# A decoder layer: the second norm's rows scaled and turned again, the up projection as one 512-column product

## The chip, the cores and the metric

The kernel runs on one core of a Trainium2 chip. The metric is the device time of one execution in microseconds, as the median of several runs. Profiled executions give a trace with every instruction of every engine: TensorE (PE in the rows, with its weight loads as PEld), VectorE (DVE), ScalarE (ACT), GpSimd (POOL) and SyncE (SP).

## What is computed

One layer of a hybrid decoder on 256 tokens of 1024 channels, in float32. Three attention branches are gated, merged, projected and added to `x`. Then comes the part that the change is in, a convolutional feed-forward block with 2 x 2816 inner channels:

```python
x = x + merged @ w_out[l]
h2 = rmsnorm(x, ffn_norm_g[l])
u = causal_depthwise_conv(h2 @ w_ffn_up[l], ffn_conv_w[l], ffn_conv_b[l])   # width 3
u_gate, u_val = jnp.split(u, 2, axis=-1)
x = x + (jax.nn.silu(u_gate) * u_val) @ w_ffn_down[l]
```

## The kernel before

**Split numbers.** TensorE multiplies rounded float32 (`F32R`). To keep the precision of float32, each operand is split into a high part (a rounded copy, made on ACT) and a low part (the rest, made on VectorE), and each product is done as three: high x high, high x low, low x high. All three are summed in PSUM. The low x low part is left out.

**Weights.** Every weight is loaded in pieces of up to 1024 columns a partition (`raw`, 6 buffers), and ACT copies it to `hi` (6 buffers, 8 in the feed-forward part). The low part `lo` is made in one of two ways: VectorE subtracts (`split_lo("dve")`), or ACT writes the negated high part and a DMA from POOL's queue adds `raw` to it (`split_lo("sum")`, the POOL rows of line 374). The second way is open to a piece only if its first use lies at least `SUMS[2]` = 5 units of work ahead (lines 339 to 347).

**Order.** The kernel is written by a planner that runs as the program is built (`Order`, lines 155 to 234). Work is a set of tasks, each a chain of stages on named engines. The planner has a cost for each instruction, takes at each step the engine that can start earliest, and there the stage with the smallest priority number among those that are due. So each engine's queue is in a fixed order, and on the chip it is worked off strictly in that order. The matmuls of the projections are the `spine`, units in a fixed sequence with priority 50; turns of rows, normalisation and evacuation are other tasks that are set between. PSUM has 4 accumulator banks (`acc`), 2 for turns (`tp`) and a larger one (`sc`). A unit that opens an accumulator waits until the fourth before it is free.

**Before the feed-forward block.** The output projection writes `x` in rows (tokens on partitions): columns 0 to 511 for both halves t = 0, 1 of the tokens, then columns 512 to 1023 of t = 0, then of t = 1. `resid` adds it to `xs`. `sums` and `rstd_task` give 1/rms of each row (`rs_h`, its power on POOL).

**The normalised input, twice.** The up projection wants channels on partitions. `turn` transposes the unscaled rows of `xs` on TensorE (`tp_hu`), and ACT and VectorE write them, times the norm's gain (a column factor), as high and low part into `T["hu"]`. The scaling by 1/rms is then by token, which lies along the free dimension: `R` holds it on all partitions, made by a product of ones with a diagonal (`tp_Rh`). Groups c < `RAW` = 3 (a group is two f of 128 channels, for gate s = 0 and value s = 1) use `T["hu"]` and multiply the accumulator by `R` afterwards (lines 979 to 981). Later groups use `T["h"]`, which `scale_task` (lines 910 to 922) makes for each k from `hu`: POOL adds the two parts (`y_h`), VectorE multiplies by `R`, ACT and VectorE split again.

**Up projection and convolution.** `up_unit` multiplies, for one f and s, k0 to k1 of the eight k; `chan` (lines 801 to 807) issues for each k three matmuls of 256 columns into one half of a bank. The first groups are cut in k so that they can start early. `conv_task` (lines 977 to 1001) then takes the accumulator: ACT scales and adds the bias (`y`), two VectorE products add the tokens one and two back, and the bank is free. SiLU (s = 0), the product of both sides and its split into `gT` follow.

**Down projection.** `dn_units` multiplies `gT` with `w_ffn_down` in 512-column matmuls (in the second half of the columns, t = 1 as two of 256), and `store` adds the result to `xs` and writes it out.

All instructions that go through the planner's wrapper have line L105 in the profile, so tiles tell them apart.

Of the kernel before, what the change touches and what calls it, by code (L numbers as in the profile page):

```python
# [11 lines left out]
F32 = mybir.dt.float32  # L12
# [3 lines left out]
AF = mybir.ActivationFunctionType  # L16
ALU = mybir.AluOpType
# [3 lines left out]
P = 128  # L21
S = 256
NT = 2
D = 1024
KT = D // P
# [9 lines left out]
NSLOT = 6  # L35
NRAW = 6
WARM = 4
RAW = 3
PRIO_SCALE = 11
CUTS = (0, 1, 2, 4, 6, 8)  # L40
LOADS = "x02 g w w x24 w X46 w X68 w"
SUMS = (4, 130, 5)
# [195 lines left out]
def tile_layer(ctx: ExitStack, tc: tile.TileContext, io, out):  # L238
    nc = tc.nc
    od = Order(nc)  # L240
    pe, act, dve, pool = od.pe, od.act, od.dve, od.pool
# [10 lines left out]
    def bank_free(tag):  # L252

        return lambda: users[tag][-BANKS[tag]]["end"] if len(users[tag]) >= BANKS[tag] else 0.0

    def bank(tag, name):
        use = {"end": None}
        users[tag].append(use)
        shape = [P, 2, 512] if tag == "sc" else [P, 512]
        return ps.tile(shape, F32, tag=tag, name=name, bufs=BANKS[tag]), use  # L260
# [11 lines left out]
    grain_of = {}  # L272
# [21 lines left out]
    at = {"unit": 0, "raw": 0, "dma": 0.0, "sw": 0.0, "lo": 0, "quiet": False}  # L294
# [44 lines left out]
    def next_lo(eng):  # L339

        for g in grains[at["lo"]:]:
            if g.get("hi", {"end": None})["end"] is None:
                return None
            if not g.get("taken"):
                if eng == "dve":
                    return g
                return g if SUMS[0] <= g["id"] < SUMS[1] and g["first"] - at["unit"] >= SUMS[2] else None

    def take_lo(eng):
        g = next_lo(eng)  # L350
# [60 lines left out]
    xs = cpool.tile([P, NT, D], F32, tag="xs", name="xs")  # L411
    small = cpool.tile([P, 3 * KT + HALF + NT], F32, tag="small", name="small")
    gcol = small[:, :3 * KT].rearrange("p (g k) -> p g k", g=3)
# [4 lines left out]
    ident = cpool.tile([P, P], F32, tag="ident", name="ident")  # L418
# [3 lines left out]
    sq, rstd = {}, {}  # L422
# [6 lines left out]
    def done(*keys):  # L429

        return lambda: [task.get(k, {"end": None}) for k in keys]
# [369 lines left out]
    def chan(o, g, cs, T_, ks, first=True, final=True):  # L801

        for n, (i, k) in enumerate(ks):
            hi, lo = g["hl"][0][:, i, cs], g["hl"][1][:, i, cs]
            pe.matmul(o, hi, T_[:, k, 0, :], start=first and n == 0, stop=False)
            pe.matmul(o, hi, T_[:, k, 1, :], start=False, stop=False)
            pe.matmul(o, lo, T_[:, k, 0, :], start=False, stop=final and n == len(ks) - 1)

    def gate_evac(c, acc, use):
        sl = sig[:, 2 * c:2 * c + 2, :]  # L810
        yield Stage("act", frees=[use])
        act.activation(sl, acc.rearrange("p (i s) -> p i s", i=2), AF.Copy)
        yield Stage("pool", done("R0", "R1"))
        pool.tensor_tensor(sl, sl, R.unsqueeze(1).to_broadcast([P, 2, S]), op=ALU.mult)
# [92 lines left out]
            dve.tensor_add(xc, acc[:, i * w:(i + 1) * w], xc)  # L907
            task[("r", t, c, i)] = {"end": od.t["dve"] + od.HOP}

    def scale_task(k):  # L910

        hi, lo = (T["h"][:, k, i, :] for i in range(2))
        a, b = (T["hu"][:, k, i, :].bitcast(F32) for i in range(2))
        y = f_["y"][:, k, :]
        yield Stage("pool", done(*[("hu", t, k // 2 * 2) for t in range(NT)]))
        pool.tensor_tensor(y, a, b, op=ALU.add)
        yield Stage("dve", done(("R", 0), ("R", 1)))
        dve.tensor_mul(y, y, R)
        yield Stage("act")
        act.activation(hi, y, AF.Copy)  # L920
        yield Stage("dve")
        dve.tensor_sub(lo, y, hi.bitcast(F32))

    def wo_units(c):
        hold = {}
        seq = [(t, k) for k in range(0, KT, 2) for t in range(NT)] if c == 0 else \
            [(t, k) for t in range(NT) for k in range(0, KT, 2)]

        def emit(t, k0):
            def go():  # L930
                if t not in hold:
                    hold[t] = bank("acc", f"acc_o{c}_{t}")
                if c == 1 and t == 0 and k0 == 0:
                    open_ffn()
                    for i in range(NT):
                        turn(xs[:, i, :], "hu", i, 1, 6, lambda k, i=i: done(("r", i, 0)), groups=((0, 2), (2, 4)))
                g = grain_of[("wo", c, k0, 0)]
                ts = slice(t * P, (t + 1) * P)
                for i in range(2):
                    mm3(hold[t][0], (T["m"][:, k0 + i, 0, ts], T["m"][:, k0 + i, 1, ts]),  # L940
                        (g["hl"][0][:, i, :], g["hl"][1][:, i, :]), k0 + i == 0, k0 + i == KT - 1)
                if k0 == KT - 2:
                    task[("r", t, c)] = od.add(resid(t, c, *hold[t]), -2 if c else 12)
                    row = xs[:, t, :]
                    if c == 0:
                        sums(row, "h", t, 14, [(0, 512, "act", done(("r", t, 0)))])
                        return
                    n = 2 if t else 1
                    sums(row, "h", t, -1, [(512, 768, "act", done(("r", t, 1, 0))),
                                           (768, 1024, "dve", done(("r", t, 1, n - 1)))])  # L950
                    at["quiet"] = t == 1
                    turn(row, "hu", t, 1, -1.5, lambda k0: done(("r", t, 1, (k0 - 4) // 2 if t else 0)),
                         groups=((4, 6), (6, 8)))
                    task["rs", "h", t] = od.add(rstd_task("h", t), -1)
                    task["R", t] = od.add(row_scale_task("h", t), 2)
                    for k in range(KT if t else 0):
                        task["h", k] = od.add(scale_task(k), PRIO_SCALE)
            return go
        for t, k0 in seq:
            unit(emit(t, k0), [("wo", c, k0, 0)], done(*[("mg", 2, ct) for ct in (k0,)]), opens=k0 == 0)  # L960
# [7 lines left out]
    def open_ffn():  # L968
        apool_cm.__exit__(None, None, None)
        f_["pool"] = ctx.enter_context(tc.tile_pool(name="fpool", bufs=1))  # L970
        for key in ("hu", "h"):
            T[key] = f_["pool"].tile([P, KT, 2, S], F32R, tag="T_" + key, name="T_" + key)
        f_["y"] = f_["pool"].tile([P, KT, S], F32, tag="y", name="y_h")
        f_["g"] = [None, None, f_["pool"].tile([P, NF - 2 * KT, 2, S], F32R, tag="gT", name="gT")]
        rings["x"] = {"pool": f_["pool"], "n": 2, "of": []}

    def conv_task(f, s, acc, use, raw):
        cw = conv[:, s * NF + f, :]
        if raw:
            yield Stage("dve", done(("R", 0), ("R", 1)))  # L980
            dve.tensor_mul(acc, acc, R)
        yield Stage("act")
        y = f_["pool"].tile([P, S], F32, tag=f"y{s}", name=f"y{s}_{f}", bufs=2)
        act.activation(y, acc, AF.Identity, scale=cw[:, 2:3], bias=cw[:, 3:4])
        yield Stage("dve", frees=[use])
        dve.scalar_tensor_tensor(y[:, 1:], acc[:, :S - 1], cw[:, 1:2], y[:, 1:], op0=ALU.mult, op1=ALU.add)
        dve.scalar_tensor_tensor(y[:, 2:], acc[:, :S - 2], cw[:, 0:1], y[:, 2:], op0=ALU.mult, op1=ALU.add)
        if s == 0:
            yield Stage("act")
            act.activation(y, y, AF.Silu)  # L990
            f_[("y", f)] = y
        else:
            yield Stage("dve", done(("u", f, 0)))
            if f % KT == 0 and f < 2 * KT:
                f_["g"][f // KT] = tpool.tile([P, KT, 2, S], F32R, tag="T8", name=f"gT{f // KT}")
            g = f_["g"][f // KT][:, f % KT]
            dve.tensor_mul(y, f_[("y", f)], y)
            yield Stage("act")
            act.activation(g[:, 0, :], y, AF.Copy)
            yield Stage("dve")  # L1000
            dve.tensor_sub(g[:, 1, :], y, g[:, 0, :].bitcast(F32))

    def up_unit(f, s, k0, k1, raw):
        def go():
            if k0 == 0:
                f_["acc", f, s] = bank("acc", f"acc_u{f}_{s}")
            acc, use = f_["acc", f, s]
            acc = acc[:, :S]
            chan(acc, grain_of[("up", f, s, 0, 0)], slice(0, P), T["hu" if raw else "h"],
                 [(k, k) for k in range(k0, k1)], k0 == 0, k1 == KT)  # L1010
            if k1 == KT:
                task[("u", f, s)] = od.add(conv_task(f, s, acc, use, raw), 10)
        unit(go, [("up", f, s, 0, 0)],
             done(*([("hu", t, k) for t in range(NT) for k in range(k0, k1, 2)] if raw else
                    [("h", k) for k in range(k0, k1)])), opens=k0 == 0)
# [198 lines left out]
```

## Time and profile before

| | us |
|---|---|
| median of 3 runs | 415.3 (414.57 to 415.33) |
| the profiled execution's own time | 414.52 |
| its span, first to last instruction | 412.7 |
| TensorE busy | 404.2 |
| VectorE busy | 302.5 |
| ACT busy | 271.6 |
| POOL busy | 60.5 |

The profiled execution is at the low end of the runs, and 1.8 us of it lie around the span. Busy shares are averages over stages. A matmul's row is longer than its distance to the next, since matmuls are pipelined; the starts tell what one costs.

### The profile page before, as it was taken

What the parts mean: (1) busy time and instruction counts of PE and PEld (TensorE: products, weight loads), DVE (VectorE), ACT (ScalarE), POOL (GpSimd) and SP (SyncE); (2) the same over time, 40 slices, a digit from 0 to 9 for tenths busy, and PEclk for the clock granted to TensorE, in tenths of its full rate; (3) what the DMA queues carried; (4) which work ended last, traced back from release to release, by engine and by line L of the source; (5) the groups of instructions that cost most, each with busy time, mean ns of one, the idle gap of its engine ahead of it and who ended that gap; (6) DMA issues with size and microseconds to landing.
All of it is one profiled execution on the core that took longest, in us unless ns stands there. A gap on an engine that the chain in (4) does not pass through costs nothing.

```text
span 412.7 us, 7727 instructions
## 1 busy us (share of the span) xinstructions
PE 404.2 (98%) x2948; PEld 381.6 (92%) x2948; DVE 302.5 (73%) x601; ACT 271.6 (66%) x449; POOL 60.5 (15%) x62
## 2 busy tenths in 40 slices
PE   7999999999999999999999899999999999999996
PEld 6999999989989999999889799999999999888986
DVE  3998996576886676468978999999997778545301
ACT  5789755879985766957676959676677776443200
POOL 0002361313233212212017000000000000000000
PEclk9999999999999999999999999999999999999999
DMA  8999987577278786687696769667789688654001
GB/s 260 369 312 343 321 231 225 128 203 192 67 179 220 194 220 170 152 245 203 191 270 162 193 143 246 192 191 217 222 253 230 214 241 239 202 185 143 1 2 51
DMA packets 97557, 82.74 MB, mean 200 GB/s; under 512 B 2928, under 2 KB 85488, under 8 KB 97520
## 3 DMA queue, kind: packets, MB, share of 16 engines
q1 hardware_dynamic: 94784, 73.33, 59.6%
q0 software_dynamic: 2448, 8.39, 11.1%
q10 hardware_dynamic: 288, 0.52, 0.5%
q8 instruction: 23, 0.38, 0.4%
q14 instruction: 14, 0.11, 0.1%
HBM read 72.80 MB, written 1.05 MB: 179 GB/s over the span
## 4 chain that ended last, share of the span: by engine, by line
PE 93%; ACT 2%; DVE 2%; DMA 1%; issue 0%; SPq 0%; ACTq 0%
PE acc_u L105 27%; PE acc_g L105 17%; PE acc_d L105 15%; PE acc_o L105 5%; PE acc_qd L105 2%; PE acc_bd L105 2%; PE acc_va L105 2%; PE acc_ba L105 2%; PE acc_kd L105 2%; PE acc_qa L105 2%; PE acc_vd L105 2%; PE acc_ka L105 2%; PE sc L105 2%; PE po L105 2%; PE acc_qm L105 1%; PE acc_mk L105 1%
## 5 line engine op out<-in xcount | busy, mean ns | idle before, releaser
L105 PE MATMUL acc_u<-T_h,hi_up 128*128 128x256 f32 x512 | 91.4, 282 | 0.0
L105 PEld LDWEIGHTS acc_u<-T_h,hi_up 128*128 128x128 f32 x512 | 78.9, 189 | 0.0
L105 PE MATMUL acc_u<-T_h,lo_up 128*128 128x256 f32 x256 | 72.1, 282 | 0.0
L105 PE MATMUL acc_g<-T_x,hi_gate 128*128 128x256 f32 x384 | 71.6, 287 | 0.0
L105 PEld LDWEIGHTS acc_g<-T_x,hi_gate 128*128 128x128 f32 x384 | 59.6, 191 | 2.1 <-issue 1.8
L105 PE MATMUL acc_d<-hi_dn,gT 128*128 128x512 f32 (+1 forms) x220 | 57.0, 348 | 0.0
L105 PE MATMUL acc_g<-T_x,lo_gate 128*128 128x256 f32 x192 | 54.2, 282 | 0.0
L105 ACT ACTIVATE hi_up<-raw_up 128x1024 fp32r<-128x1024 f32 x44 | 46.0, 1053 | 3.9 <-PE acc_o L105 1.7
L105 PEld LDWEIGHTS acc_u<-T_h,lo_up 128*128 128x128 f32 x256 | 48.4, 189 | 0.0
L105 DVE TENSOR_TENSOR lo_up<-raw_up,hi_up 128x1024 fp32r<-128x1024 f32 x39 | 47.6, 1232 | 0.0
L105 DVE SCALAR_TENSOR_TENSOR y<-acc_u,conv,y 128x255 f32<-128x255 f32 x88 | 42.2, 481 | 7.3 <-ACT y L105 5.4
L105 PEld LDWEIGHTS acc_d<-hi_dn,gT 128*128 128x128 f32 x220 | 38.5, 189 | 5.6
L105 DVE TENSOR_TENSOR lo_dn<-raw_dn,hi_dn 128x1024 fp32r<-128x1024 f32 x21 | 25.7, 1224 | 17.3 <-ACT hi_dn L105 17.3
L105 PE MATMUL acc_d<-lo_dn,gT 128*128 128x512 f32 (+1 forms) x110 | 38.3, 348 | 0.0
L105 ACT ACTIVATE hi_dn<-raw_dn 128x1024 fp32r<-128x1024 f32 x22 | 23.3, 1057 | 22.4 <-PE acc_d L105 22.4
L105 PE MATMUL acc_u<-T_hu,hi_up 128*128 128x256 f32 x192 | 34.9, 284 | 2.6 <-DVE y L105 2.6
L105 PEld LDWEIGHTS acc_g<-T_x,lo_gate 128*128 128x128 f32 x192 | 36.6, 191 | 0.0
L105 DVE TENSOR_TENSOR lo_gate<-raw_gate,hi_gate 128x1024 fp32r<-128x1024 f32 x20 | 24.1, 1220 | 13.2 <-ACT hi_gate L105 13.1
L105 PEld LDWEIGHTS acc_u<-T_hu,hi_up 128*128 128x128 f32 x192 | 29.6, 189 | 2.9 <-ACT T_h L105 2.9
L105 ACT ACTIVATE y<-acc_u,conv 128x256 f32<-128x256 f32 x44 | 24.4, 561 | 10.8 <-PE acc_u L105 10.2
L105 ACT ACTIVATE hi_gate<-raw_gate 128x1024 fp32r<-128x1024 f32 x24 | 25.0, 1055 | 6.6 <-PE acc_g L105 2.4
L105 PE MATMUL acc_u<-T_hu,lo_up 128*128 128x256 f32 x96 | 27.1, 282 | 0.0
(277 smaller groups left out, 844.8 us busy)
## 6 DMA issues: line engine op xcount, KB each, us to landing
raw_up<-w_ffn_up SPq DMA_DIRECT2D x44, 512.0 KB, 4.8
raw_gate<-w_in SPq DMA_DIRECT2D x24, 512.0 KB, 5.6
raw_dn<-w_ffn_down SPq DMA_DIRECT2D x22, 512.0 KB, 4.9
raw_wo<-w_out SPq DMA_DIRECT2D x8, 512.0 KB, 4.8
lo_up<-raw_up POOLq DMA_DIRECT2D x5, 512.0 KB, 4.7
lo_gate<-raw_gate POOLq DMA_DIRECT2D x4, 512.0 KB, 5.2
raw_vd<-w_in SPq DMA_DIRECT2D x4, 384.0 KB, 6.6
raw_qa<-w_in SPq DMA_DIRECT2D x4, 384.0 KB, 8.3
```

Of the source, the lines that this page charges most:

```text
L105: return fn(*args, **kw)
```

## The change

The scaled input `T["h"]` is no longer made from `T["hu"]`. ACT scales each row of `xs` by its 1/rms (there it is a factor for each partition) into `rows`, TensorE turns those rows a second time, and ACT and VectorE split the result from PSUM. Only group c = 0 still uses the unscaled input. In the up projection the high part of the weight is multiplied with both parts of the tokens in one 512-column matmul, which fills the bank's two halves; the low part of the weight is multiplied with the high part of the tokens into the first half. The two halves are added afterwards, by an ACT copy and a VectorE add into `u` in SBUF, from which the convolution is done. For up pieces with f > 3 the second way to a low part is open at 3 units ahead.

```diff
-RAW = 3
+RAW = 1
...
-                return g if SUMS[0] <= g["id"] < SUMS[1] and g["first"] - at["unit"] >= SUMS[2] else None
+                ahead = 3 if g["piece"]["key"][0] == "up" and g["piece"]["key"][1] > 3 else SUMS[2]
+                return g if SUMS[0] <= g["id"] < SUMS[1] and g["first"] - at["unit"] >= ahead else None
...
+    def chan_wide(o, g, T_, ks, first, final):
+
+        for n, (i, k) in enumerate(ks):
+            hi, lo = g["hl"][0][:, i, :], g["hl"][1][:, i, :]
+            pe.matmul(o, hi, T_[:, k].rearrange("p i s -> p (i s)"), start=first and n == 0, stop=False)
+            pe.matmul(o[:, :S], lo, T_[:, k, 0, :], start=False, stop=final and n == len(ks) - 1)
...
-    def scale_task(k):
-
-        hi, lo = (T["h"][:, k, i, :] for i in range(2))
-        a, b = (T["hu"][:, k, i, :].bitcast(F32) for i in range(2))
-        y = f_["y"][:, k, :]
-        yield Stage("pool", done(*[("hu", t, k // 2 * 2) for t in range(NT)]))
-        pool.tensor_tensor(y, a, b, op=ALU.add)
-        yield Stage("dve", done(("R", 0), ("R", 1)))
-        dve.tensor_mul(y, y, R)
+    def scaled_rows_task(t):
+
+        for c in range(2):
+            yield Stage("act", done(("rs", "h", t)))
+            cs = slice(c * 512, (c + 1) * 512)
+            act.activation(f_["rows"][:, t, cs], xs[:, t, cs], AF.Copy, scale=rstd["h", t][:, 0:1])
+            task["hr", t, c] = {"end": od.t["act"] + od.HOP}
+
+    def scaled_turn_task(k0):
+
+        yield Stage("pe", bank_free("tp"), done(*[("hr", t, k0 // 4) for t in range(NT)]))
+        pt, use = bank("tp", f"tp_s{k0}")
+        for i in range(2):
+            for t in range(NT):
+                pe.transpose(pt[:, i * S + t * P:i * S + (t + 1) * P],
+                             f_["rows"][:, t, (k0 + i) * P:(k0 + i + 1) * P], ident)
         yield Stage("act")
-        act.activation(hi, y, AF.Copy)
-        yield Stage("dve")
-        dve.tensor_sub(lo, y, hi.bitcast(F32))
+        for i in range(2):
+            act.activation(T["h"][:, k0 + i, 0, :], pt[:, i * S:(i + 1) * S], AF.Copy, scale=gcol[:, 1, k0 + i:k0 + i + 1])
+        yield Stage("dve", frees=[use])
+        for i in range(2):
+            hi, lo = (T["h"][:, k0 + i, part, :] for part in range(2))
+            dve.scalar_tensor_tensor(lo, pt[:, i * S:(i + 1) * S], gcol[:, 1, k0 + i:k0 + i + 1], hi.bitcast(F32),
+                                     op0=ALU.mult, op1=ALU.subtract)
...
-                    for k in range(KT if t else 0):
-                        task["h", k] = od.add(scale_task(k), PRIO_SCALE)
+                    od.add(scaled_rows_task(t), PRIO_SCALE)
+                    for k in range(0, KT if t else 0, 2):
+                        task["h", k] = task["h", k + 1] = od.add(scaled_turn_task(k), PRIO_SCALE)
...
     def conv_task(f, s, acc, use, raw):
         cw = conv[:, s * NF + f, :]
+        yield Stage("act")
+        u = f_["pool"].tile([P, S], F32, tag="u", name=f"u{s}_{f}", bufs=3)
+        act.activation(u, acc[:, S:], AF.Copy)
+        yield Stage("dve", frees=[use])
+        dve.tensor_add(u, acc[:, :S], u)
+        acc = u
         if raw:
             yield Stage("dve", done(("R", 0), ("R", 1)))
-            dve.tensor_mul(acc, acc, R)
+            dve.tensor_mul(u, u, R)
         yield Stage("act")
         y = f_["pool"].tile([P, S], F32, tag=f"y{s}", name=f"y{s}_{f}", bufs=2)
         act.activation(y, acc, AF.Identity, scale=cw[:, 2:3], bias=cw[:, 3:4])
-        yield Stage("dve", frees=[use])
+        yield Stage("dve")
...
-            acc = acc[:, :S]
-            chan(acc, grain_of[("up", f, s, 0, 0)], slice(0, P), T["hu" if raw else "h"],
-                 [(k, k) for k in range(k0, k1)], k0 == 0, k1 == KT)
+            chan_wide(acc, grain_of[("up", f, s, 0, 0)], T["hu" if raw else "h"],
+                      [(k, k) for k in range(k0, k1)], k0 == 0, k1 == KT)
```

## Rows read from the trace of the kernel before

**Rows 1.** The page's busy times and shares, and the granted clock in 40 slices.

```profile
PE 404.2 (98%) x2948; PEld 381.6 (92%) x2948; DVE 302.5 (73%) x601; ACT 271.6 (66%) x449; POOL 60.5 (15%) x62
PEclk9999999999999999999999999999999999999999
```

**Rows 2.** Chain of waits: shares by engine, then pieces (start us, us, what).

```profile
PE 93%; ACT 2%; DVE 2%; DMA 1%; issue 0%; SPq 0%; ACTq 0%
...
237.93 110.16 PE acc_u L105 x924
348.09 61.31 PE acc_d L105 x330
```

**Rows 3.** TensorE's timeline: the two places where it waits after 205 us.

```profile
233.25 0.47 PE L105 MATMUL acc_u<-T_hu,hi_up 128*128 128x256 f32 x2 [1.00 <-DVE y L105]
...
237.93 0.47 PE L105 MATMUL acc_u<-T_hu,hi_up 128*128 128x256 f32 x2 [1.59 <-DVE y L105]
```

**Rows 4.** Chain of waits: pieces of 384-column and of 512-column matmuls.

```profile
17.20 6.24 PE acc_vd L105 x36
...
212.53 2.76 PE acc_o L105 x12
...
217.12 1.39 PE acc_o L105 x6
```

**Rows 5.** Chain of waits: four transposes of 128x128.

```profile
208.91 0.44 PE tp_hu L105 x4
```

**Rows 6.** Groups by form: busy us, mean ns, then idle before them.

```profile
L105 ACT ACTIVATE y<-acc_u,conv 128x256 f32<-128x256 f32 x44 | 24.4, 561 | 10.8 <-PE acc_u L105 10.2 <-DVE acc_u L105 0.2
L105 ACT ACTIVATE gT<-y 128x256 fp32r<-128x256 f32 x22 | 9.1, 414 | 13.9 <-DVE y L105 13.9
L105 DVE TENSOR_TENSOR acc_u<-acc_u,R 128x256 f32<-128x256 f32 x12 | 4.9, 424 | 0.3 <-PE acc_u L105 0.3
L105 DVE TENSOR_TENSOR y_h<-y_h,R 128x256 f32<-128x256 f32 x8 | 4.2, 551 | 0.0
L105 ACT ACTIVATE T_x<-sig,small 128x256 fp32r<-128x256 f32 x8 | 3.6, 495 | 1.7 <-DMA sig<-x_cols 1.7
L105 DVE SCALAR_TENSOR_TENSOR T_x<-sig,small,T_x 128x256 fp32r<-128x256 f32 x8 | 3.5, 480 | 4.4 <-ACT T_x L105 4.4
L105 ACT ACTIVATE junk_h<-xs 128x512 bf16<-128x512 f32 x2 | 1.2, 623 | 0.0
```

**Rows 7.** POOL's timeline: the power for the second half's 1/rms.

```profile
220.62 1.49 POOL L105 TENSOR_TENSOR rs_h<-rs_h,mhalf 128x1 f32<-128x1 f32 x1 [1.88 <-DVE rs_h L105]
```

**Rows 8.** Engines by stretch: busy us of each, granted clock, DMA share, GB/s.

```profile
218.50:225.00 6.50, 6.50 (x58) 6.50 (x57) 6.26 (x15) 4.94 (x11) 4.62 (x6) 1.00 0.66 172
225.00:231.00 6.00, 6.00 (x52) 6.00 (x52) 5.96 (x15) 4.77 (x8) 2.65 (x3) 1.00 0.73 178
231.00:237.90 6.90, 4.33 (x35) 3.96 (x34) 6.13 (x15) 6.78 (x13) 0.00 (x0) 1.00 0.68 176
...
318.00:328.00 10.00, 10.00 (x86) 10.00 (x85) 7.79 (x13) 7.16 (x12) 0.00 (x0) 1.00 0.78 253
```

**Rows 9.** One f in the steady part: VectorE's timeline, then a low part on POOL.

```profile
314.44 1.00 DVE L105 SCALAR_TENSOR_TENSOR y<-acc_u,conv,y 128x255 f32<-128x255 f32 x2 [0.68 <-ACT y L105]
315.48 0.42 DVE L105 TENSOR_TENSOR y<-y,y 128x256 f32<-128x256 f32 x1
315.82 1.22 DVE L105 TENSOR_TENSOR lo_up<-raw_up,hi_up 128x1024 fp32r<-128x1024 f32 x1
316.95 0.42 DVE L105 TENSOR_TENSOR gT<-y,gT 128x256 fp32r<-128x256 f32 x1
...
320.16 1.00 DVE L105 SCALAR_TENSOR_TENSOR y<-acc_u,conv,y 128x255 f32<-128x255 f32 x2 [0.71 <-ACT y L105]
...
328.19 0.86 POOL L374 DMA_DIRECT2D lo_up<-raw_up  x1 [16.30 <-ACT gT L105]
```

**Rows 10.** DMA queues: packets, MB, share of 16 engines over the span.

```profile
q0 software_dynamic: 2448, 8.39, 11.1%
```

More of the change, by code (lines that the diff above doesn't have):

```diff
@@ L972, in open_ffn @@
             T[key] = f_["pool"].tile([P, KT, 2, S], F32R, tag="T_" + key, name="T_" + key)
-        f_["y"] = f_["pool"].tile([P, KT, S], F32, tag="y", name="y_h")
+        f_["rows"] = f_["pool"].tile([P, NT, D], F32, tag="rows", name="rows_h")
         f_["g"] = [None, None, f_["pool"].tile([P, NF - 2 * KT, 2, S], F32R, tag="gT", name="gT")]
```

## The prediction

> **What bounds the kernel now.** I began with the page's busy shares [rows 1]. TensorE is busy for 98% of the span and its granted clock is at the full level (2.4 GHz) in every slice, so a faster clock is nothing to look for. A busy TensorE need not be the bound, so the chain of waits came next: 93% of it is TensorE, and its two longest pieces are TensorE alone, 924 matmuls of the up projection and the 330 of the down projection [rows 2]. From there to the end nothing but matmuls counts, then one add and the last store. Every other engine matters only where TensorE stands still. After 205 us that is two places, 1.00 + 1.59 = 2.6 us, both in the up projection's start and both released by VectorE's `y` [rows 3]. So two questions decide: how much TensorE time the new matmuls take, and whether TensorE waits more or less than 2.6 us.
>
> **Matmul time.** Each of 22 x 2 outputs (f, s) takes 8 k, each k three 256-column matmuls: 352 triples. By the chain's piece a matmul takes 110.16 / 924 = 0.1192, a triple 0.3577 [rows 2]. A 512-column matmul takes 2.76 / 12 = 0.230 in the output projection, 1.39 / 6 = 0.232 at the slowest; at 384 columns 36 take 6.24, 0.173 each, which lies on the line between [rows 4]: some 0.11 us more per 256 columns, and a fixed part of about 8 ns per matmul (2 x 0.1192 - 0.230). The wide form does 512 + 256 columns: 0.230 + 0.119 = 0.349. Same columns, one fixed part less: 8 ns x 352 = 2.8 us less. With 0.232 it is 2.3; with 0.228, as far to the other side, 3.7. I take 2.8. That a 256 follows each 512 costs nothing that I can see: the down projection's second half mixes both, and the whole stage's 61.31 us is 198 x 0.230 + 132 x 0.119 = 61.2, of 198 wide and 132 narrow ones.
>
> A rule speaks against this term. The Trainium skill, "TensorE: Matmul & The Clock Gate", section "Back-to-back issue gap", gives an isolated warm matmul N / 2.4 ns and 2.5 ns more. By it a triple would save only 2.5 ns, 0.9 us in all, and the second turn below would cost more than that; the rows here show a fixed part three times as large, so I keep 2.8.
>
> **Second turn on TensorE.** 16 transposes of 128x128 are new (8 k, 2 halves of tokens). Four take 0.44 us in the chain [rows 5]: 1.8 us, all on TensorE, all in the path. The two products for R stay, since f = 0 and 1 still use unscaled rows.
>
> **The 2.6 us of waits.** TensorE stood at 232.2 and 236.3 because the accumulators of f = 2 and 3 wanted banks held by f = 0 and 1 [rows 3]. In this version a bank is freed after R's multiply, ACT's `y` and both VectorE products: 0.42, 0.56 [rows 6] and 1.00 for both [rows 9], behind other work. In the changed one ACT's copy and one add free it, some 0.41 and 0.42 by the nearest rows (gT copy, `acc_u<-acc_u,R`), and R's multiply falls behind the freeing. The last of the four accumulators ends near 231 and its bank is wanted over 4 us later. I let the whole 2.6 us go. It could stay if ACT is late, at 0 gain.
>
> **What is late next.** Raw groups fall from 3 to 1, so unscaled rows cover 32 triples = 11.2 us instead of 288 matmuls = 34 us. From 218.5 on, with the old turns and R between, group 1 (f = 2, 3) starts at 230.3, or up to 232 with all new transposes before it. It wants `h` of k = 0 to 3 then, k = 4 to 7 some 5.6 us later. The route to `h`: the second half's rstd is there at 222.1 (POOL 220.62 + 1.49, and no `y_h` add is beside it any more) [rows 7]. ACT scales two rows of 512: 0.62 each (`junk_h`, 512 wide) [rows 6], behind `T_hu` and perhaps one weight split: done at 223.5 to 225. Then by pairs of k: four transposes 0.44, ACT two of about 0.5, VectorE two of 0.48 (`T_x`, made in the same way): the first pair 2.4 us later, the next each 1.0 after, twice that when half the queue is other work. So k = 0 to 3 at 227 to 229.5, k = 6, 7 at 229 to 233.5. That is ahead of need by 1 to 4 us. TensorE's queue is in order, so a transpose placed too early also holds the matmuls behind it, and those hold all four accumulators. I charge 1.0 us for this, between 0 and the 4 us of the late rival below.
>
> Load of the two engines in this stretch: VectorE is busy for 18.35 of the 19.4 us from 218.5 to 237.9 [rows 8]. All eight `y_h` multiplies (0.55 each) and `T_h` subtractions (at 0.42, as the tensor products in [rows 9]) go, six and five of which lie before 238: 5.4 us less. Eight products from PSUM at 0.48 and four adds at 0.42 come: 5.5 more. So it stays as full as it is, with all of `h` done earlier. ACT gains two to four row scalings (0.62), four copies (0.41) and all eight `T_h`: 3 us or so more, against 1.6 + 1.2 us idle from 218.5 to 231 and next to none from 231 to 237.9. ACT is the one to watch.
>
> **Steady up projection.** Cost at nothing, and this is the cover. VectorE's cycle for one f lasts 320.16 - 314.44 = 5.72 us, of which it stands 0.71 [rows 9]. Two adds come, 0.34 each at the pitch of 315.48 to 315.82: 5.01 + 0.68 = 5.69. TensorE's new cycle is 16 x 0.349 = 5.58. So VectorE alone would be 0.11 over, but every low part that goes by ACT and DMA takes 1.13 off it (315.82 to 316.95). That was done at 328.19, and 16.30 us of POOL's idle time before, and the change lets it happen with three units of lead where five were asked. One in nine f closes the gap. ACT is busy for 7.16 of 10 us there [rows 8], 4.1 of 5.72; two copies make it 4.9. Products that now read `u` from SBUF I leave at 0.48: `T_x`, from SBUF with a column factor, takes 0.48 as well. DMA: 0.78 of the engines' time is taken there [rows 8]; the software queue has 11.1% of the span for its 8.39 MB, that is 45.8 us / 16 = 2.9 us for each half MB [rows 10]. Six more in the 90 us of f = 4 to 21 would be 17 us, 0.97 in place of 0.78. It fits, not by much.
>
> **Sum**, for the profiled execution: 414.52 - 2.8 + 1.8 - 2.6 + 1.0 = 411.9 (the span, 412.7, and 1.8 around it that don't change). It is 0.8 below the median of the runs (415.3, lowest 414.57), so against that median 412.7.
>
> **Rivals.**
> Late `h`. ACT is full from 231 to 238 and gets the row scalings, the copies and the turns' first parts; if k = 0 to 3 land at 233 and not before 230.5 to 232, TensorE stands for 1 to 3 us, and again before k = 4. With 4 us of waits in place of my 1.0: 415.7, no change. For it: a third of the cover. Against it: 1 to 4 us of reserve.
>
> VectorE as the bound, the slower side. Place: f = 4 to 21. If its 0.71 us of waits for ACT stay (each output now makes two more hops between ACT and VectorE), its cycle is 5.72 + 0.68 = 6.40, 0.82 over TensorE's; over 18 f that is 14.8 us. From there each low part moved to the DMA takes back 1.13; with nine, 4.6 are left. On top of the forecast that gives 417.3. It decides as soon as (waits - 1.13 x moved parts per f) exceeds -0.11. Against it: the waits of 0.71 are VectorE waiting for TensorE's pace, and shrink when it is loaded.
>
> Small gain per triple: the pitch of 256 columns could be set by the weight loads beside it (TensorE's load rows are busy for 92% [rows 1]), and a wide one that needs fewer loads could still be held up by them. If only a third of the 8 ns goes, a triple takes 0.355 and 0.9 us are saved, not 2.8: 412.7 + 1.9 = 414.6, no change. Against it: three column counts on one line, which loads would bend. The formula of the Trainium skill, "TensorE: Matmul & The Clock Gate" (section as above), comes to the same 0.9.
>
> The waits are not removed: the banks come free earlier but TensorE still stands for 2.6 us in all, for a weight's low part; then -2.8 + 1.8 = -1.0: 414.3.
>
> **Chances.** Forecast 0.60, with its own range 410.8 (waits 0, saving 3.7) to 414.2 (waits 2, saving 2.3). Late `h` 0.17, VectorE 0.11, small gain 0.05, waits stay 0.07. Within 0.2% (0.8 us, about what a measurement of this kernel can tell from none) is 414.5 to 416.1. Faster: nearly all of the forecast, most of the last, a little of the others: 0.68. Same: most of late `h` and of small gain, 0.17. Slower: VectorE, and late `h` beyond 4.4 us of waits: 0.15. Range 410.6 to 416.8: the lower end just below the own range; the upper short of VectorE's full price, which leaves out about 1 in 10 there.
>
> **What the changed profile would show.** Wide triples at 0.349; 352 512-column rows for `acc_u`. Sixteen more transposes between 222 and 233. The waits of TensorE after 205 us: no `acc_u` held by VectorE's `y`, and at most about 1 us for `rows` or `T_h`. VectorE 95 to 99% busy from 250 to 340, more low parts on POOL's queue, TensorE without idle there. The down projection stays at 61.3. Wrong is the forecast if the triple takes 0.355, if TensorE waits over 3 us in the turn's stretch, or if any wait for `lo_up` or `acc_u` shows after 245.

## The result, and the profile after

The changed kernel takes 411.68 us in the median (411.55 to 411.97, 4 runs), the kernel before 414.94 beside it: ratio 0.9931, 95% interval 0.9912 to 0.9950. In a second measurement it was 411.79 and 0.9930 (0.9912 to 0.9948). That is 3.3 us less; 412.7 was forecast.

First the page: busy times, and the granted clock [rows 1 before].

```profile
PE 403.1 (98%) x2612; PEld 365.6 (89%) x2612; DVE 307.4 (75%) x627; ACT 285.8 (70%) x499; POOL 54.5 (13%) x56
PEclk9999999999999999999999999999999999999999
```

Then the chain of waits, its last pieces (start us, us, what) [rows 2 before].

```profile
PE 92%; DMA 3%; ACT 2%; DVE 2%; issue 1%; SPq 0%; DVEq 0%
...
223.64 0.44 PE tp_s L105 x4
224.07 0.22 PE tp_Rh L105 x2
224.30 2.80 PE acc_u L105 x16
227.10 0.87 PE tp_s L105 x8
227.97 5.63 PE acc_u L105 x32
233.60 0.44 PE tp_s L105 x4
234.04 111.09 PE acc_u L105 x632
345.13 61.31 PE acc_d L105 x330
```

TensorE's busy time is down by only 1.1 us, since the busy rows overlap; the chain tells more. It runs from the turns to the end through TensorE alone, where before it crossed ACT and VectorE from 221 to 238. TensorE has no wait at all after 205 us: both of [rows 3] are gone. The new transposes are there, 0.44 + 0.87 + 0.44 = 1.75 us. 632 matmuls, 316 pairs of a wide and a narrow one, take 111.09 us: 0.3516 a pair, where the kernel before took 0.3577 for three narrow ones. The down projection has the same 61.31 us as before.

A good ruler for everything below is the **up stage**, from the start of the first product for R to the start of the first down matmul: 347.92 - 218.35 = 129.57 us before, 344.97 - 218.62 = 126.35 after, 3.22 less. What lies ahead of it moves between the profiled executions (its start lies between 217.76 and 219.61 us in the kernels below, those of the gates apart) and has no part in the change; the down projection that follows takes the same time.

Engines by stretch, after [rows 8 before].

```profile
218.50:225.00 6.50, 6.50 (x43) 5.85 (x42) 4.67 (x15) 5.26 (x13) 0.57 (x1) 1.00 0.64 157
225.00:231.00 6.00, 6.00 (x39) 5.33 (x39) 5.93 (x10) 6.00 (x12) 0.00 (x0) 1.00 0.72 209
231.00:237.90 6.90, 6.90 (x43) 6.12 (x42) 6.37 (x17) 6.73 (x13) 0.89 (x1) 1.00 0.56 140
...
318.00:328.00 10.00, 10.00 (x59) 8.72 (x58) 9.64 (x19) 7.10 (x15) 0.02 (x1) 1.00 0.82 220
```

VectorE (third busy number) has 16.97 us of work in the first 19.4, 1.4 less than before; ACT, 17.99 in place of 16.49. In the stretch from 318 VectorE is near full, 9.64 of 10 against 7.79; over 250 to 340 us it is 85.59 of 90 against 81.35. The kernel before had a stretch as full: 57.87 of 60 us from 240 to 300, without a wait of TensorE. The groups behind it [rows 6 before]:

```profile
L105 ACT ACTIVATE rows_h<-xs,rs_h 128x512 f32<-128x512 f32 x4 | 2.7, 728 | 0.0
L105 ACT ACTIVATE T_h<-tp_s,small 128x256 fp32r<-128x256 f32 x8 | 3.3, 477 | 0.0
L105 DVE SCALAR_TENSOR_TENSOR T_h<-tp_s,small,T_h 128x256 fp32r<-128x256 f32 x8 | 3.4, 475 | 0.0
L105 ACT ACTIVATE u<-acc_u 128x256 f32<-128x256 f32 x44 | 16.2, 371 | 3.8 <-PE acc_u L105 3.7
L105 DVE TENSOR_TENSOR u<-acc_u,u 128x256 f32<-128x256 f32 x44 | 17.6, 417 | 0.0
L105 ACT ACTIVATE y<-u,conv 128x256 f32<-128x256 f32 x44 | 25.2, 593 | 1.5 <-DVE u L105 1.4
```

### The profile page after: what moved, and what is told of

Its sections match the earlier page's. It is cut to its first block, busy times and chain, and to the rows that moved or that the text cites. A ratio compares the mean times of both kernels' runs of the same rounds, so it can differ in the third digit from the quotient of the medians.

```text
span 409.8 us, 7075 instructions
## 1 busy us (share of the span) xinstructions
PE 403.1 (98%) x2612; PEld 365.6 (89%) x2612; DVE 307.4 (75%) x627; ACT 285.8 (70%) x499; POOL 54.5 (13%) x56
## 4 chain that ended last, share of the span: by engine, by line
PE 92%; DMA 3%; ACT 2%; DVE 2%; issue 1%; SPq 0%; DVEq 0%
PE acc_u L105 30%; PE acc_g L105 16%; PE acc_d L105 15%; PE acc_o L105 5%; PE acc_qd L105 2%; PE acc_bd L105 2%; PE acc_ba L105 2%; PE acc_va L105 2%; PE acc_kd L105 2%; PE sc L105 2%; PE po L105 2%; DMA sig<-mem_cols 2%; PE acc_vd L105 2%; PE acc_qm L105 1%; PE acc_mk L105 1%; PE acc_bm L105 1%
## 5 line engine op out<-in xcount | busy, mean ns | idle before, releaser
L105 PE MATMUL acc_u<-T_h,hi_up 128*128 128x512 f32 x320 | 112.7, 395 | 0.0
L105 PE MATMUL acc_u<-T_h,lo_up 128*128 128x256 f32 x320 | 90.3, 282 | 0.0
L105 PEld LDWEIGHTS acc_u<-T_h,hi_up 128*128 128x128 f32 x320 | 60.1, 188 | 14.1
L105 PEld LDWEIGHTS acc_u<-T_h,lo_up 128*128 128x128 f32 x320 | 60.2, 188 | 0.0
L105 DVE TENSOR_TENSOR lo_up<-raw_up,hi_up 128x1024 fp32r<-128x1024 f32 x37 | 44.9, 1217 | 1.4 <-ACT hi_up L105 1.4
L105 DVE SCALAR_TENSOR_TENSOR y<-u,conv,y 128x255 f32<-128x255 f32 x88 | 42.2, 481 | 2.8 <-ACT y L105 0.8
L105 ACT ACTIVATE y<-u,conv 128x256 f32<-128x256 f32 x44 | 25.2, 593 | 1.5 <-DVE u L105 1.4
L105 PEld LDWEIGHTS acc_d<-lo_dn,gT 128*128 128x128 f32 x110 | 20.8, 189 | 2.8
L105 PE MATMUL acc_o<-hi_wo,mT 128*128 128x512 f32 x64 | 20.9, 396 | 0.0
L105 POOL TENSOR_TENSOR sig<-sig,R 128x512 f32<-128x512 f32 x12 | 16.0, 1331 | 34.9 <-ACT sig L105 34.9
```

Of the source, the lines that this page charges most:

```text
L105: return fn(*args, **kw)
```

## The experiments

The first theory, made after the result, was the prediction's sum with measured sizes: 2.2 us less for the pairs (0.3577 - 0.3515, 352 times), 2.6 for the bank waits, 1.8 more for the turns. Its rival: the waits went because VectorE was relieved, not because banks are freed earlier. Four kernels take the change apart.

**Three narrow matmuls in the changed kernel.** Everything else stays.

```diff
-            pe.matmul(o, hi, T_[:, k].rearrange("p i s -> p (i s)"), start=first and n == 0, stop=False)
+            pe.matmul(o[:, :S], hi, T_[:, k, 0, :], start=first and n == 0, stop=False)
+            pe.matmul(o[:, S:], hi, T_[:, k, 1, :], start=False, stop=False)
```

> The changed kernel with three 256-column matmuls per k again (high weight x high tokens into the first half of the bank, high x low into the second, low x high into the first); everything else as changed. Theory (the gain is 2.2 us of matmul pitch plus 2.6 us of bank waits less 1.8 us of transposes): 352 triples at 0.3577 in place of the measured 0.3515 give 2.2 us more, 411.7 + 2.2 = 413.9, with TensorE still without a wait after 205 us. Rival (the pitch saves 0.9 us or nothing, all else came from the waits): 411.7 to 412.6.

Measured: 412.71, ratio to the kernel before 0.9958 (0.9945 to 0.9970). Its chain, the longest piece:

```profile
230.71 115.62 PE acc_u L105 x972
```

That is 0.3569 for three, against 0.3516 for the pair: 5.3 ns. The up stage is 128.26 us, 1.91 over the changed kernel's. By the stage, which no jitter ahead of it touches, the wide form is worth 1.9 us; the medians, measured at different times, say 1.0. TensorE has no wait, as the theory said. The time lies nearer to the rival's (412.6 at most) than to the theory's 413.9, the stage nearer to the theory's 2.2 than to 0.9.

**A copy that frees the bank early, in the kernel before.**

```diff
+        yield Stage("act", frees=[use])
+        u = f_["pool"].tile([P, S], F32, tag="u", name=f"u{s}_{f}", bufs=3)
+        act.activation(u, acc, AF.Copy)
+        acc = u
         if raw:
             yield Stage("dve", done(("R", 0), ("R", 1)))
-            dve.tensor_mul(acc, acc, R)
+            dve.tensor_mul(u, u, R)
...
-        yield Stage("dve", frees=[use])
+        yield Stage("dve")
```

> The kernel before with one edit: ACT copies each up accumulator to SBUF, which frees its bank at once, and R's multiply and the convolution work on the copy. 256-column matmuls, old scaled input, three raw groups. Theory (the two waits of 1.00 and 1.59 us came from banks held too long): no wait of TensorE after 205 us, 414.9 - 2.6 = 412.3. Rival (the waits went because VectorE lost the y_h work and two groups' multiplies by R): the waits stay, 414.9, or more since ACT has 44 copies more to do.

Measured: 419.32, ratio 1.0114 (1.0099 to 1.0130), slower by 4.8 us. TensorE's waits after 190 us (in total, times, longest):

```profile
PE acc_u L105 <- DVE T_h L105: 3.7, 2, 2.9
PE acc_u L105 <- ACT T_h L105: 0.6, 1, 0.6
```

No bank is waited for. So the theory is right that an early release ends those two waits, but its time, 412.3, is missed by 7 us. TensorE runs on to the groups that need `T_h`, and the last of those stand in VectorE's order at 257 to 261, where in the kernel before they were made by 241. That is the planner's order, not more work on VectorE: it is busy for 303.0 us in all, against 302.5 before. Whether the early release would gain with `T_h` put earlier was not run. Part of the price is the clock, as in the next kernel: the granted clock is 0.77 from 260 to 270, after TensorE was busy for 6.24 of the 10 us before, and the 750 matmuls after the last wait take 91.17 us, 1.7 more than 250 triples at 0.3577.

**The wide product alone.** `conv_task` and the up projection as changed, `scale_task` and `RAW = 3` as before; `u` has 6 buffers in place of 3.

```diff
+        yield Stage("act")
+        u = f_["pool"].tile([P, S], F32, tag="u", name=f"u{s}_{f}", bufs=6)
+        act.activation(u, acc[:, S:], AF.Copy)
+        yield Stage("dve", frees=[use])
+        dve.tensor_add(u, acc[:, :S], u)
+        acc = u
...
+            chan_wide(acc, grain_of[("up", f, s, 0, 0)], T["hu" if raw else "h"],
+                      [(k, k) for k in range(k0, k1)], k0 == 0, k1 == KT)
```

> The kernel before with the wide product and the sum of its halves alone (u with 6 buffers): T_h still made on POOL, VectorE and ACT from the unscaled parts, three raw groups, lead 5. Theory: both gains without the transposes' price, 414.9 - 2.2 - 2.6 = 410.1, so below the changed kernel. Rival (VectorE, which keeps the y_h work and gets 44 adds, is what holds TensorE in the first 20 us): waits of 2.6 us or more after 218 us, 412.7 to 415.

Measured: 425.69, ratio 1.0254 (1.0234 to 1.0274), slower by 11 us; the up stage is 140.02. The greatest wait, and three stretches:

```profile
PE acc_u L105 <- DVE T_h L105: 8.6, 3, 7.3
```

```profile
240.00:250.00 10.00, 10.00 (x59) 8.73 (x58) 9.64 (x17) 7.32 (x14) 0.00 (x0) 1.00 0.67 194
250.00:260.00 10.00, 8.45 (x46) 6.64 (x44) 9.45 (x21) 7.96 (x14) 0.00 (x0) 1.00 0.62 174
260.00:270.00 10.00, 2.66 (x6) 1.55 (x6) 9.21 (x23) 4.04 (x9) 0.00 (x0) 0.68 0.00 0
```

Neither time held (410.1, and 412.7 to 415); the waits that the rival expected are there, and larger. VectorE is over 92% busy all the way while TensorE falls to 2.66 us of 10, and the granted clock, after that idling, to 0.68 in the last stretch (a mean of its two levels). So the idling is paid for again. A pair that starts at the lower level takes 0.64 us (271.53 to 272.17) in place of 0.35:

```profile
271.53 0.63 PE L105 MATMUL acc_u<-T_h,hi_up 128*128 128x512 f32 x1
...
272.17 0.63 PE L105 MATMUL acc_u<-T_h,hi_up 128*128 128x512 f32 x1
```

In the chain, the 249 pairs after the last wait take 1.9 us more than at 0.3516:

```profile
270.09 89.48 PE acc_u L105 x498
```

The faster half of the change, taken alone, is the worst of these four kernels.

**The second turn alone.** `scaled_rows_task` and `scaled_turn_task` in place of `scale_task`; 256-column matmuls, `RAW = 3`, banks held as before.

```diff
-                    for k in range(KT if t else 0):
-                        task["h", k] = od.add(scale_task(k), PRIO_SCALE)
+                    od.add(scaled_rows_task(t), PRIO_SCALE)
+                    for k in range(0, KT if t else 0, 2):
+                        task["h", k] = task["h", k + 1] = od.add(scaled_turn_task(k), PRIO_SCALE)
```

> The kernel before with the second turn alone: rows scaled on ACT and transposed again, split from PSUM; 256-column matmuls, three raw groups, banks held as before. Theory: 16 transposes at 0.11 more and the bank waits unchanged, 414.9 + 1.8 = 416.7 with about 2.6 us of waits for acc_u. Rival (relief of VectorE removes the waits): 414.9 + 1.8 - 2.6 = 414.1.

Measured: 413.49, ratio 0.9975 (0.9961 to 0.9989), faster although TensorE has 1.75 us more to do. The up stage is 128.84. TensorE's waits after 205 us:

```profile
PE acc_u L105 <- DVE y L105: 0.3, 1, 0.3
```

A bank is still held until the convolution's second product, and 2.3 of the 2.6 us of waits are gone: the rival is right that they can go without an early release. VectorE's work from 218.5 to 237.9 is 4.94 + 5.96 + 6.65 = 17.55 us against 18.35 [rows 8], with all eight `T_h` in it instead of five. Part of that is POOL's doing. In the kernel before, VectorE's instructions beside the `y_h` adds are stretched:

```profile
222.84 0.75 DVE L105 TENSOR_SCALAR diag_h<-ident,rs_h 128x128 f32<-128x128 f32 x1
223.51 1.77 DVE L105 TENSOR_TENSOR lo_up<-raw_up,hi_up 128x1024 fp32r<-128x1024 f32 x1
```

In the changed kernel the same two take 0.28 and 1.22. The power on POOL takes 0.57 in place of 1.49 [rows 7], but no add lay beside it in the kernel before (they ran to 218.7 and again from 222.08), and a `lo_up` of VectorE lies beside it in both; no run shows what made it slow.

That VectorE's relief is the cause is argued, not shown: the second turn also takes POOL out of the way to `T_h`. And VectorE was not alone in being late. In the chain of the kernel before, the 16.8 us from 221.1 to the end of the second wait are 8.3 of ACT and 7.1 of VectorE; in this kernel ACT has 10.9 of 16.1.

So the second theory (capacity): VectorE's load between 218 and 270 us decides whether TensorE waits, and the second turn is what makes room. Against it stands that the planner only put the work in a bad order. Four more kernels.

**T_h ahead of the convolution, in the wide kernel.**

```diff
-PRIO_SCALE = 11
+PRIO_SCALE = 6
```

> The wide product alone in the kernel before (as wide_only), with one number changed: the priority of the tasks that make T_h is 6 in place of 11, so they go ahead of the convolution (10). In wide_only the last three T_h stood in VectorE's order behind 23 us of other work and TensorE waited 8.6 us for them. Order theory (VectorE has room, the planner left T_h too late): T_h is there by 245, waits under 3 us, 411 to 414. Capacity theory (VectorE has more work than time between 218 and 270 with the y_h route and the adds): the wait moves to accumulators or low parts and stays above 5 us, 418 or more.

Measured: 418.97, ratio 1.0098 (1.0071 to 1.0126); the up stage is 135.20. These are TensorE's waits, the engines from 240 to 250, and the subtractions for `T_h` (ns, then first and last start), which are through by 235.1:

```profile
PE acc_u L105 <- ACT hi_up L105: 3.7, 1, 3.7
PE acc_u L105 <- DVE u L105: 2.3, 3, 0.9
PE acc_u L105 <- ACT gT L105: 0.3, 1, 0.3
```

```profile
240.00:250.00 10.00, 10.00 (x50) 8.69 (x49) 7.21 (x15) 5.94 (x13) 0.88 (x1) 0.83 0.46 107
```

```profile
L105 DVE TENSOR_TENSOR T_h<-y_h,T_h x8: 414/422/426, 228.2 to 234.7; 128x256 fp32r<-128x256 f32 x8
```

Of the 10.45 us that the wide kernel's up stage was over the one before, this order takes away 4.8; 5.6 are left, and the waits moved to accumulators and weights, 6.3 us in all. That is what the capacity theory expected. But it isn't proof: 3.7 of the 6.3 is for a weight's high part on ACT, and VectorE is busy for only 7.21 us of 10 from 240 to 250. How much a third order would take away was not run.

**The `y_h` multiplies on POOL, in the wide kernel.**

```diff
-        yield Stage("dve", done(("R", 0), ("R", 1)))
-        dve.tensor_mul(y, y, R)
+        yield Stage("pool", done(("R", 0), ("R", 1)))
+        pool.tensor_tensor(y, y, R, op=ALU.mult)
```

> wide_only with the eight multiplies of y_h by R on POOL in place of VectorE (priority 11 as before). It takes 8 x 0.42 to 0.55 = 4 us off VectorE in the stretch and leaves TensorE's work as in wide_only. Capacity theory: the wait shrinks by about those 4 us or more, from 10.7 over the kernel before to 6 or less, 415 to 421. Order theory: the last subtractions for T_h are as late as they were, 423 to 426.

Measured: 423.43, ratio 1.0208 (1.0185 to 1.0232). The wait for `T_h` is still 7.1 us, its last subtractions still start at 266.7: with priority 11 they stay late. Its up stage is 138.54, 1.5 less than with the multiplies on VectorE. That is what the order theory expected (423 to 426): 4 us less work on VectorE bring little while the order keeps `T_h` late. It leaves open what they bring in a better order.

**Three raw groups in the changed kernel** (`u` with 6 buffers).

```diff
-RAW = 1
+RAW = 3
```

> The changed kernel with three groups on the unscaled input again in place of one (u with 6 buffers, which three groups need). Eight more multiplies by R (0.42 each) on VectorE, T_h wanted 22 us later. Theory (VectorE's load between 218 and 260 decides, the cover is not short): no wait for T_h, and 3.4 us more on a VectorE that is 95 to 98% busy: waits of 0 to 3 us, 411.7 to 414.7. Rival (the short cover costs something in the changed kernel, such as the order that it forces): 410.5 to 411.5.

Measured: 415.46, ratio 1.0013 (1.0000 to 1.0026); the up stage is 130.11, 3.76 over the changed kernel's. `T_h` is not waited for, as the theory said, but the time is above its 414.7. What TensorE waits for is `DVE u`, the add that frees a bank (2.4 us in 6 places), in these stretches among others:

```profile
250.00:260.00 10.00, 8.86 (x48) 7.03 (x46) 8.98 (x17) 6.76 (x14) 0.00 (x0) 1.00 0.58 165
260.00:270.00 10.00, 9.01 (x48) 7.34 (x48) 9.58 (x19) 6.56 (x12) 0.00 (x0) 1.00 0.54 155
```

Eight multiplies by R of 0.42, 3.4 us on VectorE, cost 3.8 us of TensorE. The step from three raw groups to one is a part of the gain in its own right as soon as the adds are there. VectorE's share alone doesn't tell it: the changed kernel has 9.65 and 9.58 of 10 in the same two stretches and no wait.

Set beside the wide product alone (140.02), this kernel (130.11) also shows what the second turn is worth where the adds are: 9.9 us. The two differ in the second turn and in the lead rule, which the next run shows to bring nothing in the changed kernel.

**Five units of lead everywhere, in the changed kernel.**

```diff
-                ahead = 3 if g["piece"]["key"][0] == "up" and g["piece"]["key"][1] > 3 else SUMS[2]
+                ahead = SUMS[2]
```

> The changed kernel with five units of lead asked for again everywhere before a low part may go by ACT and DMA. Theory (the steady stretch lives near VectorE's limit: 5.69 us of work in 5.62 per f): fewer than the seven low parts go by DMA, and TensorE gets waits of 0.5 to 3 us after 245, 412.2 to 414.7. Rival (VectorE has room by the lead that it builds up): 411.7, no waits.

Measured: 410.83, ratio 0.9918 (0.9896 to 0.9939), no wait, the up stage 126.35 as in the changed kernel. Two low parts of the up weights go by DMA, not seven. The rival holds, and the waits that the theory expected are not there: the lead rule is worth nothing here. Where the missing VectorE time comes from is seen at the start of the down projection, first this kernel, then the changed one:

```profile
355.00:365.00 10.00, 10.00 (x45) 8.16 (x44) 8.39 (x9) 5.11 (x5) 0.00 (x0) 1.00 0.84 271
```

```profile
355.00:365.00 10.00, 10.00 (x45) 8.16 (x44) 4.91 (x4) 4.85 (x5) 0.00 (x0) 1.00 0.88 328
```

VectorE carries its backlog past the end of the up projection, 8.39 of 10 us in place of 4.91, into a stage where it has room.

Last, a control, the missing step between the second turn and the changed kernel, and an attempt to go on.

**The changed kernel again.**

> The changed kernel unaltered, to have it on the same chip as the next three: 411.7, 126.35 us from R's first product to the down projection, no wait of TensorE.

Measured: 411.79, ratio 0.9930 (0.9912 to 0.9948), the up stage 126.35, no wait.

**The second turn with one raw group**: the kernel of the second turn alone, and this.

```diff
-RAW = 3
+RAW = 1
```

> The kernel before with the second turn and one raw group: 256-column matmuls, no copy and no add, banks held until the convolution's second product as before, lead 5. Capacity theory (VectorE's load between 218 and 260 made the waits, not the time that a bank is held): no waits after 205 us, TensorE's work as in narrow_in_after, so about 1.0 us over the changed kernel, 412.7. Rival (the early release of the banks is needed): 2 us of waits for banks, 414.7.

Measured: 413.98, ratio 0.9985 (0.9973 to 0.9998). The up stage is 128.85, as with three groups (128.84): without the adds the eight multiplies by R are free. One wait of 0.4 us for a bank is left, not the rival's 2, though the time lies between the two expectations (412.7 and 414.7). From here to the narrow form of the changed kernel (128.26) it is 0.59: the wait, and triples of 0.3569 in place of 0.3577. The copies, the adds and the early release lie between the two, and the lead rule.

**The wide product in the gates too**, on top of the changed kernel, once with the lead rule and once with five units everywhere.

```diff
-                if i == 0 and h == 0:
-                    hold["a"] = bank("acc", f"acc_g{c}")
-                acc, use = hold["a"]
-                chan(acc[:, i * S:(i + 1) * S], grain_of[("gate", c, 0, i * P)], slice(0, P), T["x"],
-                     [(k, k) for k in range(4 * h, 4 * h + 4)], h == 0, h == 1)
+                if h == 0:
+                    hold[i] = bank("acc", f"acc_g{c}_{i}")
+                acc, use = hold[i]
+                chan_wide(acc, grain_of[("gate", c, 0, i * P)], T["x"],
+                          [(k, k) for k in range(4 * h, 4 * h + 4)], h == 0, h == 1)
```

> The changed kernel with the wide product in the gate projection too (192 triples; a bank for each half instead of one for both, ACT copies one half of the bank, VectorE adds the other, POOL multiplies by R as before). TensorE theory: the 5.3 ns a triple that narrow_in_after showed give 192 x 5.3 = 1.0 us, 410.7. Rival (twice as many banks and 24 more adds hold TensorE among the attention's tasks): 412 or more, with waits for acc_g between 30 and 190 us.

> As wide_gates, with five units of lead asked for everywhere. Since the lead rule moved nothing in lead5_in_after (up projection 126.34 us against 126.35), the same time as wide_gates within 0.3 us.

Measured: 424.65, ratio 1.0238 (1.0204 to 1.0273), and 423.33, 1.0222 (1.0191 to 1.0252), by the ratios the same within their intervals. TensorE's waits in the first:

```profile
PE tp_qa L105 <- DVE t_qa L105: 3.6, 1, 3.6
PE po L105 <- ACT pT L105: 3.1, 2, 1.9
PE tp_qd L105 <- DVE t_qd L105: 2.1, 2, 1.9
```

None of them is for `acc_g`, so the rival had the sign and the wrong place. The gates' matmuls fill TensorE between the attention's tasks, whose normalisation and softmax run on VectorE and ACT. With shorter gates and 24 adds more on VectorE, TensorE arrives at `tp_qa` 3.6 us before its rows are there. Which of the two does it, or the planner's new order, no run tells apart. No version beats the changed kernel by more than the measurement can tell.

## Why the prediction was right

The time, its sign and the range came out. That is in part luck: a saving put too high and waits charged that never came cancel in part, and the step on the bank waits had its size right although the cause that it named is only one of two. By its steps, in us of the up stage:

| step | predicted | measured |
|---|---|---|
| wide product | -2.8 | -2.2 (352 times 0.3577 to 0.3516) |
| 16 transposes | +1.8 | +1.75 |
| old bank waits | -2.6 | -2.9 |
| new waits | +1.0 | 0 |
| sum | -2.6 | -3.3 by the terms, -3.2 in the stage |

The bank waits are 2.6 us of idle time in the rows but cost 2.9: the starts around them lie 1.28 and 1.88 us apart in place of 0.12 (231.97 to 233.25, 236.05 to 237.93), since the last row before an idle stretch runs longer than its distance to the next would be.

**Wide product.** The mis-sized term. With 0.119 for the narrow matmul the wide one takes 0.3516 - 0.119 = 0.2326 here, the slow end of the pitches in [rows 4] (0.232) and not their middle; the prediction's own 2.3 for that end is what came. Against the triples of the kernel before the pair saves 6.1 ns, where 8 were expected. 5.3 of them are the form of the product (against three narrow ones in the changed kernel); the other 0.8 the changed kernel's narrow form has as well, and what makes them no run shows. As an estimate by the rule of the Trainium skill ("TensorE: Matmul & The Clock Gate", "Back-to-back issue gap", 2.5 ns of fixed part) the saving is 0.9 us; the measured 1.9 for the product's form lies midway between that and the 2.8.

**Bank waits.** The step said that a copy and an add free the bank early, and that this ends the waits. An early release does end them: with the copy alone no bank is waited for. But the second turn ends most of them too, with the banks held as before (0.3 left), and the early release without the second turn makes the kernel 4.8 us slower. So the change holds two remedies for the same waits, and the prediction counted on one. What frees a bank was late behind other work on ACT and VectorE. The prediction's own balance of VectorE came out even in this stretch, where 1.4 us less were measured; it left out that POOL's adds stretch VectorE's instructions beside them (1.77 in place of 1.22).

**New waits.** None, but the reserve is thinner than the 1 to 4 us that were claimed. Predicted were k = 0 to 3 at 227 to 229.5 and k = 6, 7 by 233.5; measured were about 232.2 and 238.5. The first pair came at 226.7, as predicted; then ACT split three weights (225.43 to 228.7) before the next pair's high parts, and the later pairs fell further behind. VectorE's products for `T_h`, and the TensorE matmuls that want k = 2 and k = 6:

```profile
231.42 1.65 DVE L105 SCALAR_TENSOR_TENSOR T_h<-tp_s,small,T_h 128x256 fp32r<-128x256 f32 x4
237.62 0.87 DVE L105 SCALAR_TENSOR_TENSOR T_h<-tp_s,small,T_h 128x256 fp32r<-128x256 f32 x2
```

```profile
232.03 0.40 PE L105 MATMUL acc_u<-T_h,hi_up 128*128 128x512 f32 x1
...
232.74 0.39 PE L105 MATMUL acc_u<-T_h,hi_up 128*128 128x512 f32 x1
...
238.79 0.40 PE L105 MATMUL acc_u<-T_h,hi_up 128*128 128x512 f32 x1
```

The third product (k = 4) starts at about 232.2, so k = 2 and 3 are ready about then, half a microsecond ahead of 232.74. The last two are through at 238.49, with k = 6 wanted at 238.79. The late rival's condition (k = 0 to 3 at 233) was missed by less than 1 us, and the reserve was tenths.

**Steady up projection.** Cost at nothing, rightly. VectorE's cycle there, without a low part by DMA:

```profile
299.68 0.42 DVE L105 TENSOR_TENSOR y<-y,y 128x256 f32<-128x256 f32 x1
...
305.24 0.42 DVE L105 TENSOR_TENSOR y<-y,y 128x256 f32<-128x256 f32 x1
```

5.56 us in this cycle, against 5.62 on TensorE (16 x 0.3516): the two are level, 5.69 and 5.58 were predicted. The relief by DMA that the prediction counted on was not needed; lead and the down stage take the difference up.

**VectorE as the bound.** The slower rival did not come true, but it lies next door: with the old route to `h`, or with three raw groups, TensorE waits for results of VectorE among others, and the up stage is 10.4 over the kernel before or 3.8 over the changed one. It sat earlier than the prediction had it, in the first 50 us or so of the stage and not in the steady stretch. How much of the 10.4 is VectorE's capacity and how much the planner's order stays open: another order took 4.8 away.

## What to carry to other kernels

Two halves of a change on a loaded engine are not two gains: here the second turn is worth 0.7 us alone, the wide product costs 10.4 alone, and together, with one raw group, they gain 3.2. Where TensorE waits for a bank, look at what the engine that should free it still has ahead of that in its queue, before shortening the time that the bank is held; a full engine alone is no sign, since VectorE was as full in stretches without a wait. Where matmuls serve as cover for another stage's work, as the gates seem to do here, making them shorter can cost time.

## What the runs showed of the hardware

A 512-column matmul in place of two of 256 saved 5.3 ns in a row of alternating widths. An ACT copy of 128x256 took 371 ns from PSUM, written as float32, and 411 to 414 from SBUF, written as rounded float32; with column factor and bias 561 from PSUM [rows 6] and 593 from SBUF, in the same form. VectorE's products took the same 0.48 us from either. VectorE's instructions beside POOL's adds took longer (1.77 against 1.22, 0.75 against 0.28); the add beside that 1.77 took 1.71 on POOL, the shortest one 0.73. In the wide kernel TensorE's granted clock fell to a mean of 0.68 in a stretch in which it was busy for 2.66 of 10 us, and a pair took 0.64 us at the lower level against 0.35.
